# RMSNorm with swish: units of 8 rows in place of 4, one unit per loop round

## The chip, the cores and the metric

The kernel runs on one core of a Trainium2 chip. A core has engines that run side by side, each with its own stream of instructions: TensorE (PE), VectorE (DVE), ScalarE (ACT), GpSimd (POOL) and SyncE (SP). They meet through semaphores. 16 DMA engines move data between the device memory (HBM) and the on-chip memory (SBUF, 128 partitions). The metric is device time in microseconds (us). Lower is better.

## The reference

```python
def reference(x, gamma, eps):            # x: 16 x 1024 x 512 float32, gamma: 512
    rms = np.sqrt(np.mean(x ** 2, axis=-1, keepdims=True) + eps)
    x_norm = x / rms * gamma
    return x_norm * (1.0 / (1.0 + np.exp(-x_norm)))
```

Each of the 16,384 rows of 512 numbers is divided by its own root mean square, multiplied by gamma, and sent through swish (x times its sigmoid). Input and output are 33.55 MB each.

## The kernel before

**Tiling.** Each of the 128 partitions holds 128 rows, so "row r" below means row r of every partition: 128 × 2 KB. SBUF has room for 96 rows in a ring buffer `xb`, and the work is done in place there: a row is loaded, normed, swished and stored from the same spot. Rows 96 to 127 take the place of rows 0 to 31. A *unit* is `cn` = 4 rows, and there are K = 32 of them.

**The five streams.**

- *SyncE* issues all DMAs from one queue, in an order written out by hand (`order`). First the loads of rows 0 to 79 (ten pieces, named by their first row), gamma among them. Then it waits until the load of row 64 has landed ("landed", L167) and issues the store of rows 0 to 31 (L122), then the load of rows 80 to 95 (L116). It waits until that store has finished ("stored") and issues the loads of rows 96 to 127. It waits for the landing of row 112, and issues the other five stores: 32 to 63, 64 to 79, 80 to 95, 96 to 119, 120 to 127. Each store also waits until enough units are finished: `s_swish` must have reached ceil(last row / cn). SyncE takes its instructions in order, so a store that waits holds those behind it.
- *TensorE* multiplies nothing. It carries signals (L177): for unit k it waits for the loads that begin in the unit, and for a sign that the small buffers of unit k - 2 are free, and then counts up `s_land`.
- *ScalarE*, per unit: it waits for `s_land`, squares and sums three of the four rows (one ACTIVATE and one accumulator read each, L219), and then swishes a whole *earlier* unit in one instruction (L227), once VectorE has normed it. It squares two units ahead of the unit that it swishes. The last two units are swished in a single instruction after the loop, which adds 2 to `s_swish` at once.
- *VectorE*, per unit: it sums the squares of the fourth row (L245), and then norms the four rows of the unit before: row × rstd × gamma, one instruction per row (L253).
- *GpSimd*, per unit: it adds eps to the four means (L185), and raises them to the power -1/2 (L190): `rstd`.

So the chain of a unit is: load, squares on ScalarE, the last sum on VectorE, rstd on GpSimd, norms on VectorE, swish on ScalarE, store.

**Loops.** ScalarE and VectorE each run a hardware loop with two units per round (15 rounds); row addresses come from registers, which each round computes anew (fused register operations, L215). GpSimd runs a loop with two units per round as well. Waits inside loops count their semaphore down again (`take`: wait for n, subtract n), so that the waited value stays constant.

Of the kernel before, what the change touches and what calls it, by code (L numbers as in the profile page):

```python
# [9 lines left out]
def kernel(  # L10
# [7 lines left out]
    nc = tc.nc  # L18
    P = nc.NUM_PARTITIONS
    AF = mybir.ActivationFunctionType  # L20
    ALU = mybir.AluOpType
    fp32 = mybir.dt.float32
# [3 lines left out]
    R, D = xf.shape  # L26

    groups = [32, 48, 16, 32]
    ring = 96
# [6 lines left out]
    order += [("stored", 0), ("load", 96), ("load", 112), ("load", 122)]  # L36
    order += [("landed", 112)] + [("store", a) for a in (32, 64, 80, 96, 120)]
    early = 2
    cn = 4

    first = [sum(groups[:g]) for g in range(len(groups))]
    rows_each = sum(groups)
# [6 lines left out]
        assert sum(n for _, n in pieces) == rows_each  # L49

    K = rows_each // cn
    U = 2
    rounds = (K - 2) // U
    assert U * rounds == K - 2
    load_at = {a: t for t, (a, _) in enumerate(loads)}
    store_at = {a: t for t, (a, _) in enumerate(stores)}
    ends = [-(-(a + n) // cn) for a, n in stores]
# [1 line left out]
    inv_d = 1.0 / float(D)  # L59
    eps_f = float(eps)  # L60
# [4 lines left out]
    def sbuf(name, shape, dt=fp32):  # L65
        return nc.alloc_sbuf_tensor(name, shape, dt).ap()

    xb = sbuf("xb", [P, ring, D])
    gamma4 = sbuf("gamma4", [P, D])
    gamma_sb = sbuf("gamma_sb", [P, D])  # L70
    neg_half = sbuf("neg_half", [P, cn])
    ms = [sbuf(f"ms{u}", [P, cn]) for u in range(U)]
    aeps = [sbuf(f"aeps{u}", [P, cn]) for u in range(U)]
    rstd = [sbuf(f"rstd{u}", [P, cn]) for u in range(U)]
    junk = [
        nc.alloc_psum_tensor(f"junk{i}", [P, D], fp32).ap() for i in range(U * (cn - 1))
    ]
    junk_v = [sbuf(f"junk_v{u}", [P, D]) for u in range(U)]

    ld = [nc.alloc_semaphore(f"ld{t}") for t in range(len(loads))]  # L80
    st = [nc.alloc_semaphore(f"st{t}") for t in range(2)]
# [4 lines left out]
    s_land = nc.alloc_semaphore("s_land")  # L86
    s_acc = nc.alloc_semaphore("s_acc")
    s_sum = nc.alloc_semaphore("s_sum")
    s_free = nc.alloc_semaphore("s_free")
    s_eps = nc.alloc_semaphore("s_eps")  # L90
    s_rstd = nc.alloc_semaphore("s_rstd")
    s_norm = nc.alloc_semaphore("s_norm")
# [2 lines left out]
    def need(ins, sem, value):  # L95
        return ins.wait_op(sem, value, "sem-ge")

    def take(queue, sem, n=1):
        queue.wait_ge(sem, n).then_inc(sem, -n)  # L99
# [9 lines left out]
    def buf(piece):  # L109
        a, n = piece  # L110
        at = a % ring
        assert at + n <= ring, piece
        return xb[:, at : at + n, :]

    def load(t):
        return nc.sync.dma_start(  # L116
            out=buf(loads[t]), in_=dram(xf, loads[t])
        ).then_inc(ld[t], 16)
# [25 lines left out]
    for t in range(early):  # L144
        ins = load(t).ins
        assert here[-1] is ins or here[-1].name == ins.name
        here.pop()
        at = next(
            i for i, other in enumerate(entry)
            if other.engine == mybir.EngineType.SP  # L150
            and isinstance(other, mybir.InstDrain)
        )
        entry.insert(at, ins)
    for what, a in order[early:]:
# [4 lines left out]
        elif what == "gamma":  # L159
            need(  # L160
                nc.sync.dma_start(
                    out=gamma4[0:P:32, :], in_=gamma.partition_broadcast(4)
# [10 lines left out]
    for k in range(K):  # L173
        for t, (a, n) in enumerate(loads):
            if k * cn <= a < (k + 1) * cn:
                nc.tensor.wait_ge(ld[t], 16)
        nc.tensor.wait_ge(s_free, max(0, k - U + 1)).then_inc(s_land, 1)  # L177

    nc.gpsimd.memset(gamma4, 0.0).then_inc(s_zero, 1)  # L179
    nc.gpsimd.memset(neg_half, -0.5).then_inc(s_half, 1)  # L180
    nc.gpsimd.wait_ge(s_half, 1)

    def rsqrt(u):
        take(nc.gpsimd, s_sum)
        nc.gpsimd.tensor_scalar(  # L185
            out=aeps[u], in0=ms[u], scalar1=eps_f, scalar2=None, op0=ALU.add,
        ).then_inc(s_eps, 1)
        take(nc.gpsimd, s_eps)
        nc.gpsimd.sem_inc(s_free, 1)
        nc.gpsimd.tensor_tensor(  # L190
            out=rstd[u], in0=aeps[u], in1=neg_half, op=ALU.pow
        ).then_inc(s_rstd, 1)

    rsqrt(0)
    rsqrt(1)
    with nc.gpsimd.Fori(0, rounds, 1):
        for j in range(U):
            rsqrt((2 + j) % U)

    flat = xb.rearrange("p n d -> p (n d)")  # L200
    size = cn * D

    def unit_of(i):
        at = nc.s_assert_within(
            i % (ring * D), 0, ring * D - size,
            skip_runtime_bounds_check_because="whole units, and the ring is whole units",
        )
        return flat[:, bass.ds(at, size)]

    def row_of(unit, r):  # L210
        return unit[:, r * D : (r + 1) * D]

    def addresses(queue, aps):
        for ap in aps:
            queue.lower_ap(ap)  # L215

    def square(u, rows):
        for j in range(cn - 1):
            acc = nc.scalar.activation(  # L219
                out=junk[u * (cn - 1) + j], in_=rows[j], func=AF.Square,  # L220
                scale=inv_d**0.5, accum_out=ms[u][:, j : j + 1],
            )
        acc.then_inc(s_acc, 1)

    def swish(rows, n=1):
        take(nc.scalar, s_norm, n)
        nc.scalar.activation(out=rows, in_=rows, func=AF.Silu).then_inc(s_swish, n)  # L227

    nc.scalar.preload_act_table_set("silu_and_others")  # L229
    take(nc.scalar, s_land, 2)  # L230
    for k in range(2):
        square(k, [xb[:, k * cn + j, :] for j in range(cn)])
    with nc.scalar.Fori(0, rounds * U * size, U * size) as i:
        new = [unit_of(i + (j + 2) * size) for j in range(U)]
        old = [unit_of(i), unit_of(i + size)]
        sq_rows = [[row_of(unit, r) for r in range(cn - 1)] for unit in new]
        addresses(nc.scalar, old + sum(sq_rows, []))
        for j in range(U):
            take(nc.scalar, s_land)
            square((2 + j) % U, sq_rows[j])  # L240
            swish(old[j])
    swish(buf(((K - 2) * cn, 2 * cn)), 2)

    def sums(u, row):
        nc.vector.scalar_tensor_tensor(  # L245
            out=junk_v[u], in0=row, scalar=inv_d, in1=row,
            op0=ALU.mult, op1=ALU.mult, accum_out=ms[u][:, cn - 1 : cn],
        ).then_inc(s_sum, 1)

    def norm(u, rows):  # L250
        take(nc.vector, s_rstd)
        for j in range(cn):
            ins = nc.vector.scalar_tensor_tensor(  # L253
                out=rows[j], in0=rows[j], scalar=rstd[u][:, j : j + 1],
                in1=gamma_sb, op0=ALU.mult, op1=ALU.mult,
            )
        ins.then_inc(s_norm, 1)

    take(nc.vector, s_acc, 2)
    for k in range(2):  # L260
        sums(k, xb[:, k * cn + cn - 1, :])
    need(nc.vector.stream_shuffle(gamma_sb, gamma4, [0] * 32), s_gld, 16).then_inc(  # L262
        s_gamma, 1
    )
    nc.vector.wait_ge(s_gamma, 1)
    norm(0, [xb[:, j, :] for j in range(cn)])
    with nc.vector.Fori(0, rounds * U * size, U * size) as i:
        of_unit = [unit_of(i + (j + 1) * size) for j in range(U + 1)]
        rows = [[row_of(unit, r) for r in range(cn)] for unit in of_unit]
        addresses(nc.vector, sum(rows[:U], []) + rows[U][cn - 1 :])  # L270
        for j in range(U):
            take(nc.vector, s_acc)
            sums((2 + j) % U, rows[j + 1][cn - 1])
            norm((1 + j) % U, rows[j])
    norm((K - 1) % U, [buf(((K - 1) * cn + j, 1))[:, 0, :] for j in range(cn)])


# [33 lines left out]
```

## Time and profile before

| | us |
|---|---|
| median of three runs | 160.26 (159.98 to 161.02) |
| the profiled execution | 160.24 |
| its span, first to last instruction | 158.9 |
| VectorE busy | 107.8 (68%), 194 instructions |
| ScalarE busy | 119.5 (75%), 224 instructions |
| GpSimd busy | 56.7 (36%), 70 instructions |

The largest groups, by line, engine and operation; `out<-in` names the tiles, then come the count, the busy us and the mean ns of one, and the idle time ahead of them with what ended it:

```profile
L253 DVE SCALAR_TENSOR_TENSOR xb<-xb,rstd,gamma_sb 128x512 f32 (+1 forms) x128 | 87.4, 746 | 0.9 <-DVEq L99 0.9
L227 ACT ACTIVATE xb<-xb (+1 forms) x31 | 60.7, 1959 | 6.5 <-ACTq L99 6.5
L219 ACT ACTIVATE junk<-xb 128x512 f32 (+1 forms) x96 | 55.7, 580 | 6.0 <-ACTq L99 6.0
L190 POOL TENSOR_TENSOR rstd<-aeps,neg_half 128x4 f32<-128x4 f32 x32 | 38.7, 1208 | 8.4 <-POOLq L99 8.4
```

DVEq, ACTq, POOLq and SPq are the engines' sequencers, which take the waits; L99 is `take`. The busy tenths divide the span into 40 slices of 4 us; each digit is the busy share of a slice, 9 for 90% or more. Times within the span are counted from its first instruction.

### The profile page before, as it was taken

How to read it: one execution, taken by the hardware profiler on the slowest of the kernel's cores; microseconds unless marked ns; L12 is line 12 of the kernel's file. 1: busy time of each engine (PE TensorE's matmuls, PEld its weight loads, DVE VectorE, ACT ScalarE, POOL GpSimd, SP SyncE). 2: the span in 40 equal slices, each digit the busy share in tenths (PEclk: the TensorE clock that was granted, in tenths of full speed). 3: DMA queues.
4: the chain of work that ended last, by engine and by line, in shares of the span. 5: the costliest groups of instructions: out<-in, count | busy, mean ns of one | idle time of the engine just before them, and what ended most of it. 6: DMA issues, size and time to landing. Idle time of an engine off the chain costs nothing. (4 is left out here: it accounts for less than half of the span.)

```text
span 158.9 us, 1059 instructions
## 1 busy us (share of the span) xinstructions
DVE 107.8 (68%) x194; ACT 119.5 (75%) x224; POOL 56.7 (36%) x70
## 2 busy tenths in 40 slices
DVE  0017989889999999999988999999999970000000
ACT  3174799999999999999999999999999617000000
POOL 1007444444445545555444444554555500000000
DMA  7999999999899969979999899798989999999975
GB/s 258 452 415 450 412 507 412 396 437 487 363 415 542 528 264 528 478 297 412 396 487 429 383 424 601 317 528 379 412 388 404 503 404 404 470 396 520 445 338 214
DMA packets 2744, 67.12 MB, mean 422 GB/s; under 512 B 308, under 2 KB 308, under 8 KB 312
## 3 DMA queue, kind: packets, MB, share of 16 engines
q1 hardware_dynamic: 2744, 67.12, 98.6%
HBM read 33.56 MB, written 33.55 MB: 422 GB/s over the span
## 5 line engine op out<-in xcount | busy, mean ns | idle before, releaser
L253 DVE SCALAR_TENSOR_TENSOR xb<-xb,rstd,gamma_sb 128x512 f32 (+1 forms) x128 | 87.4, 746 | 0.9 <-DVEq L99 0.9
L227 ACT ACTIVATE xb<-xb (+1 forms) x31 | 60.7, 1959 | 6.5 <-ACTq L99 6.5
L219 ACT ACTIVATE junk<-xb 128x512 f32 (+1 forms) x96 | 55.7, 580 | 6.0 <-ACTq L99 6.0
L190 POOL TENSOR_TENSOR rstd<-aeps,neg_half 128x4 f32<-128x4 f32 x32 | 38.7, 1208 | 8.4 <-POOLq L99 8.4
L185 POOL TENSOR_SCALAR aeps<-ms 128x4 f32<-128x4 f32 x32 | 17.3, 541 | 60.4 <-POOLq L99 60.4
L245 DVE SCALAR_TENSOR_TENSOR junk_v<-xb 128x512 f32 (+1 forms) x32 | 22.1, 692 | 21.5 <-DVEq L99 21.5
L219 ACT ACTIVATION_READ_ACCUMULATOR junk<-xb 128x1 f32 x96 | 17.9, 186 | 0.0
L229 ACT ACT_TABLE_LOAD x1 | 1.3, 1283 | 1.9 <-PEq L63 1.9
L245 DVE DVE_READ_ACCUMULATOR junk_v<-xb 128x1 f32 x32 | 2.6, 82 | 0.0
L179 POOL MEMSET gamma<- 128x512 f32 x1 | 0.5, 524 | 1.5 <-POOLq L63 1.5
L262 DVE STREAM_SHUFFLE gamma_sb<-gamma 128x512 f32<-128x512 f32 x1 | 0.7, 715 | 0.0
L292 POOL MEMSET const-float32-0.0<- 128x1 f32 x1 | 0.1, 98 | 0.2 <-issue 0.2
L292 POOL MEMSET const-bfloat16-1.0<- 128x1 bf16 x1 | 0.1, 101 | 0.0
L292 POOL MEMSET const-uint8-127<- 128x1 uint8 x1 | 0.1, 101 | 0.0
L180 POOL MEMSET neg_half<- 128x4 f32 x1 | 0.1, 101 | 0.0
L292 POOL MEMSET const-float32-1.0<- 128x1 f32 x1 | 0.1, 98 | 0.0
L262 DVE LOAD_MASK_SELECT gamma_sb<-gamma x1 | 0.0, 11 | 0.0
## 6 DMA issues: line engine op xcount, KB each, us to landing
xb<-in_x_dram SPq DMA_DIRECT2D x4, 4096.0 KB, 29.8
out_dram<-xb SPq DMA_DIRECT2D x2, 4096.0 KB, 34.3
xb<-in_x_dram SPq DMA_DIRECT2D x3, 2048.0 KB, 13.9
out_dram<-xb SPq DMA_DIRECT2D x1, 6144.0 KB, 28.1
xb<-in_x_dram SPq DMA_DIRECT2D x1, 2816.0 KB, 43.0
xb<-in_x_dram SPq DMA_DIRECT2D x1, 2560.0 KB, 25.1
xb<-in_x_dram SPq DMA_DIRECT2D x2, 1024.0 KB, 5.7
out_dram<-xb SPq DMA_DIRECT2D x1, 2048.0 KB, 24.9
```

The source lines that it names most:

```text
L179: nc.gpsimd.memset(gamma4, 0.0).then_inc(s_zero, 1)
L180: nc.gpsimd.memset(neg_half, -0.5).then_inc(s_half, 1)
L185: nc.gpsimd.tensor_scalar(out=aeps[u], in0=ms[u], scalar1=eps_f, scalar2=None, op0=ALU.add,).then_inc(s_eps, 1)
L190: nc.gpsimd.tensor_tensor(out=rstd[u], in0=aeps[u], in1=neg_half, op=ALU.pow).then_inc(s_rstd, 1)
L219: acc = nc.scalar.activation(out=junk[u * (cn - 1) + j], in_=rows[j], func=AF.Square, scale=inv_d**0.5, accum_out=ms[u][:, j : j + 1],)
L227: nc.scalar.activation(out=rows, in_=rows, func=AF.Silu).then_inc(s_swish, n)
L229: nc.scalar.preload_act_table_set("silu_and_others")
L245: nc.vector.scalar_tensor_tensor(out=junk_v[u], in0=row, scalar=inv_d, in1=row, op0=ALU.mult, op1=ALU.mult, accum_out=ms[u][:, cn - 1 : cn ...
L253: ins = nc.vector.scalar_tensor_tensor(out=rows[j], in0=rows[j], scalar=rstd[u][:, j : j + 1], in1=gamma_sb, op0=ALU.mult, op1=ALU.mult,)
L262: need(nc.vector.stream_shuffle(gamma_sb, gamma4, [0] * 32), s_gld, 16).then_inc(s_gamma, 1)
L292: nc = _bacc.Bacc("TRN2", target_bir_lowering=False, num_devices=1)
```

## The change

A unit becomes 8 rows (`cn` = 8, K = 16), and a loop round of ScalarE and VectorE handles one unit instead of two. Of the 8 rows, ScalarE squares six and VectorE two (`own` = 2); of the first unit, four each (`own_first` = 4). A swish covers 8 rows, 128x4096; the one after the loop still covers the last two units, now 16 rows, 128x8192. The hand-written order and the pieces of the loads and stores stay as they are, and so does the rule ceil(last row / cn) for a store's wait.

GpSimd's loop is written out: 16 pairs of instructions, each waiting on a constant. `rstd` becomes one tile for all rows, which VectorE reads at an address from a register. The sums of unit 0 go to one small tile, `ms[0]`, and those of all later units to the other, `ms[1]`. The sign that a unit's small buffers are free is now GpSimd's `s_eps`, which TensorE reads without counting it down. VectorE's loop starts one unit earlier, with the first unit's norms inside it; per round it computes addresses with nine fused register operations instead of five, ScalarE with three instead of four. One new wait is on ScalarE's own second square, ahead of the second unit.

```diff
-    cn = 4
+    cn = 8
+    own = 2
+    own_first = 4
...
-    rstd = [sbuf(f"rstd{u}", [P, cn]) for u in range(U)]
+    rstd = sbuf("rstd", [P, rows_each])
...
-        nc.tensor.wait_ge(s_free, max(0, k - U + 1)).then_inc(s_land, 1)
+        nc.tensor.wait_ge(s_eps, 0 if k < 2 else k).then_inc(s_land, 1)
...
-    rsqrt(0)
-    rsqrt(1)
-    with nc.gpsimd.Fori(0, rounds, 1):
-        for j in range(U):
-            rsqrt((2 + j) % U)
+    for k in range(K):
+        need(
+            nc.gpsimd.tensor_scalar(
+                out=aeps[k % 2], in0=ms[min(k, 1)], scalar1=eps_f, scalar2=None, op0=ALU.add,
+            ),
+            s_sum, k + 1,
+        ).then_inc(s_eps, 1)
+        need(
+            nc.gpsimd.tensor_tensor(
+                out=rstd[:, k * cn : (k + 1) * cn], in0=aeps[k % 2], in1=neg_half, op=ALU.pow
+            ),
+            s_eps, k + 1,
+        ).then_inc(s_rstd, 1)
...
-    take(nc.scalar, s_land, 2)
-    for k in range(2):
-        square(k, [xb[:, k * cn + j, :] for j in range(cn)])
-    with nc.scalar.Fori(0, rounds * U * size, U * size) as i:
-        new = [unit_of(i + (j + 2) * size) for j in range(U)]
-        old = [unit_of(i), unit_of(i + size)]
-        sq_rows = [[row_of(unit, r) for r in range(cn - 1)] for unit in new]
-        addresses(nc.scalar, old + sum(sq_rows, []))
-        for j in range(U):
-            take(nc.scalar, s_land)
-            square((2 + j) % U, sq_rows[j])
-            swish(old[j])
+    take(nc.scalar, s_land)
+    square(ms[0], junk[cn - own_first :], [xb[:, j, :] for j in range(cn - own_first)])[1].then_inc(s_two, 1)
+    nc.scalar.wait_ge(s_two, 1)
+    take(nc.scalar, s_land)
+    square(ms[1], junk, [xb[:, cn + j, :] for j in range(cn - own)])
+    with nc.scalar.Fori(0, (K - 2) * size, size) as i:
+        new, old = unit_of(i + 2 * size), unit_of(i)
+        sq_rows = [row_of(new, r) for r in range(cn - own)]
+        old_rows = row_of(old, 0, cn)
+        addresses(nc.scalar, [old_rows] + sq_rows)
+        take(nc.scalar, s_land)
+        square(ms[1], junk, sq_rows)
+        swish(old_rows)
     swish(buf(((K - 2) * cn, 2 * cn)), 2)
...
-    take(nc.vector, s_acc, 2)
-    for k in range(2):
-        sums(k, xb[:, k * cn + cn - 1, :])
+    take(nc.vector, s_acc)
+    sums(ms[0], [xb[:, j, :] for j in range(cn - own_first, cn)])
...
-    norm(0, [xb[:, j, :] for j in range(cn)])
-    with nc.vector.Fori(0, rounds * U * size, U * size) as i:
...
-        for j in range(U):
-            take(nc.vector, s_acc)
-            sums((2 + j) % U, rows[j + 1][cn - 1])
-            norm((1 + j) % U, rows[j])
+    with nc.vector.Fori(0, (K - 1) * size, size) as i:
+        new, old = unit_of(i + size), unit_of(i)
+        rows = [row_of(old, r) for r in range(cn)]
+        sum_rows = [row_of(new, r) for r in range(cn - own, cn)]
...
+        factors = [rstd[:, j : rows_each - cn + j + 1][:, bass.ds(at, 1)] for j in range(cn)]
+        addresses(nc.vector, rows + sum_rows + factors)
+        take(nc.vector, s_acc)
+        sums(ms[1], sum_rows)
+        norm(rows, factors)
```

More of the change, by code (lines that the diff above doesn't have):

```diff
@@ L51 @@
     K = rows_each // cn
-    U = 2
-    rounds = (K - 2) // U
-    assert U * rounds == K - 2
     load_at = {a: t for t, (a, _) in enumerate(loads)}
@@ L71 @@
     neg_half = sbuf("neg_half", [P, cn])
-    ms = [sbuf(f"ms{u}", [P, cn]) for u in range(U)]
-    aeps = [sbuf(f"aeps{u}", [P, cn]) for u in range(U)]
-    rstd = [sbuf(f"rstd{u}", [P, cn]) for u in range(U)]
+    ms = [sbuf(f"ms{u}", [P, cn]) for u in range(2)]
+    aeps = [sbuf(f"aeps{u}", [P, cn]) for u in range(2)]
+    rstd = sbuf("rstd", [P, rows_each])
     junk = [
-        nc.alloc_psum_tensor(f"junk{i}", [P, D], fp32).ap() for i in range(U * (cn - 1))
+        nc.alloc_psum_tensor(f"junk{i}", [P, D], fp32).ap() for i in range(cn)
     ]
-    junk_v = [sbuf(f"junk_v{u}", [P, D]) for u in range(U)]
+    junk_v = [sbuf(f"junk_v{j}", [P, D]) for j in range(own_first)]
     ld = [nc.alloc_semaphore(f"ld{t}") for t in range(len(loads))]
@@ L88 @@
     s_sum = nc.alloc_semaphore("s_sum")
-    s_free = nc.alloc_semaphore("s_free")
+    s_two = nc.alloc_semaphore("s_two")
     s_eps = nc.alloc_semaphore("s_eps")
@@ L181 @@
     nc.gpsimd.wait_ge(s_half, 1)
[L183 to L186, printed above, removed]
-        ).then_inc(s_eps, 1)
[L188 to L191, printed above, removed]
-        ).then_inc(s_rstd, 1)
-    rsqrt(0)
-    rsqrt(1)
-    with nc.gpsimd.Fori(0, rounds, 1):
-        for j in range(U):
-            rsqrt((2 + j) % U)
+    for k in range(K):
[4 more added lines that the diff above has]
+            s_sum, k + 1,
+        ).then_inc(s_eps, 1)
+        need(
[3 more added lines that the diff above has]
+            s_eps, k + 1,
+        ).then_inc(s_rstd, 1)
     flat = xb.rearrange("p n d -> p (n d)")
@@ L203, in unit_of @@
     def unit_of(i):
-        at = nc.s_assert_within(
+        return nc.s_assert_within(
             i % (ring * D), 0, ring * D - size,
@@ L207, in unit_of, with row_of @@
         )
-        return flat[:, bass.ds(at, size)]
-    def row_of(unit, r):
-        return unit[:, r * D : (r + 1) * D]
+    def row_of(unit, r, n=1):
+        return flat[:, r * D : ring * D - size + (r + n) * D][:, bass.ds(unit, n * D)]
     def addresses(queue, aps):
@@ L215, in addresses, with square @@
             queue.lower_ap(ap)
[L217 to L221, printed above, removed]
-            )
-        acc.then_inc(s_acc, 1)
+    def square(sums, dummies, rows):
+        done = []
+        for j in range(len(rows)):
+            done.append(
+                nc.scalar.activation(
+                    out=dummies[j], in_=rows[j], func=AF.Square,
+                    scale=inv_d**0.5, accum_out=sums[:, j : j + 1],
+                )
+            )
+        done[-1].then_inc(s_acc, 1)
+        return done
     def swish(rows, n=1):
@@ L229, with sums, norm @@
     nc.scalar.preload_act_table_set("silu_and_others")
-    take(nc.scalar, s_land, 2)
-    for k in range(2):
-        square(k, [xb[:, k * cn + j, :] for j in range(cn)])
-    with nc.scalar.Fori(0, rounds * U * size, U * size) as i:
-        new = [unit_of(i + (j + 2) * size) for j in range(U)]
-        old = [unit_of(i), unit_of(i + size)]
-        sq_rows = [[row_of(unit, r) for r in range(cn - 1)] for unit in new]
-        addresses(nc.scalar, old + sum(sq_rows, []))
-        for j in range(U):
-            take(nc.scalar, s_land)
-            square((2 + j) % U, sq_rows[j])
-            swish(old[j])
-    swish(buf(((K - 2) * cn, 2 * cn)), 2)
[L244 to L250, printed above, removed]
+    take(nc.scalar, s_land)
[11 more added lines that the diff above has]
+        swish(old_rows)
+    swish(buf(((K - 2) * cn, 2 * cn)), 2)
+    def sums(to, rows):
+        n = len(rows)
+        for j in range(n):
+            ins = nc.vector.scalar_tensor_tensor(
+                out=junk_v[j], in0=rows[j], scalar=inv_d, in1=rows[j],
+                op0=ALU.mult, op1=ALU.mult, accum_out=to[:, cn - n + j : cn - n + j + 1],
+            )
+        ins.then_inc(s_sum, 1)
+    def norm(rows, factors):
         take(nc.vector, s_rstd)
@@ L253, in norm @@
             ins = nc.vector.scalar_tensor_tensor(
-                out=rows[j], in0=rows[j], scalar=rstd[u][:, j : j + 1],
+                out=rows[j], in0=rows[j], scalar=factors[j],
                 in1=gamma_sb, op0=ALU.mult, op1=ALU.mult,
@@ L265 @@
     nc.vector.wait_ge(s_gamma, 1)
-    norm(0, [xb[:, j, :] for j in range(cn)])
-    with nc.vector.Fori(0, rounds * U * size, U * size) as i:
-        of_unit = [unit_of(i + (j + 1) * size) for j in range(U + 1)]
-        rows = [[row_of(unit, r) for r in range(cn)] for unit in of_unit]
-        addresses(nc.vector, sum(rows[:U], []) + rows[U][cn - 1 :])
-        for j in range(U):
-            take(nc.vector, s_acc)
-            sums((2 + j) % U, rows[j + 1][cn - 1])
-            norm((1 + j) % U, rows[j])
-    norm((K - 1) % U, [buf(((K - 1) * cn + j, 1))[:, 0, :] for j in range(cn)])
+    with nc.vector.Fori(0, (K - 1) * size, size) as i:
+        new, old = unit_of(i + size), unit_of(i)
+        rows = [row_of(old, r) for r in range(cn)]
+        sum_rows = [row_of(new, r) for r in range(cn - own, cn)]
+        at = nc.s_assert_within(
+            i // D, 0, rows_each - cn,
+            skip_runtime_bounds_check_because="whole units",
+        )
+        factors = [rstd[:, j : rows_each - cn + j + 1][:, bass.ds(at, 1)] for j in range(cn)]
[3 more added lines that the diff above has]
+        norm(rows, factors)
+    k = K - 1
+    norm(
+        [buf((k * cn + j, 1))[:, 0, :] for j in range(cn)],
+        [rstd[:, k * cn + j : k * cn + j + 1] for j in range(cn)],
+    )
 _INS = ['x', 'gamma', 'eps']
```

## The prediction

> **What bounds the kernel now.** I read the page's busy tenths first, then the DMA queue, then SyncE's waits.
>
> ```profile
> DVE  0017989889999999999988999999999970000000
> ACT  3174799999999999999999999999999617000000
> ...
> DMA  7999999999899969979999899798989999999975
> ...
> DMA packets 2744, 67.12 MB, mean 422 GB/s; under 512 B 308, under 2 KB 308, under 8 KB 312
> ...
> q1 hardware_dynamic: 2744, 67.12, 98.6%
> ```
>
> The DMA engines are full from the first slice to the last but one (98.6% of 16 engines), while VectorE and ScalarE stop at 134 us of 158.9. So the span is 67.12 MB through a queue that never runs empty, and compute can only matter where it lets the queue run empty. That happens where SyncE holds a store back:
>
> ```profile
> SPq L167 <- DMA xb<-in_x_dram: 66.3, 2, 42.1
> SPq L122 <- ACT xb L227: 36.2, 4, 21.8
> SPq L171 <- DMA out_dram<-xb: 24.5, 1, 24.5
> ```
>
> The second line is stores waiting for swishes. Whether such a wait hurts is told by the backlog behind it. SyncE's timeline and the DMA view of single windows (issue, then us to landing) give it: the store of rows 80 to 95 is issued at 103.76 and lands 35.8 us later, at 139.5. The next store (rows 96 to 119) is issued at 125.90, 11.8 us before its first packet can move: the packet records show the first engine taking it up at 137.65. The last (rows 120 to 127) is issued at 133.99 and lands at 158.9.
>
> ```profile
> 48.20 0.35 SPq L122 DMA_DIRECT2D out_dram<-xb  x1
> 48.59 23.65 SPq L116 DMA_DIRECT2D xb<-in_x_dram  x4
> 96.51 37.81 SPq L122 DMA_DIRECT2D out_dram<-xb  x5
> ```
>
> ```profile
> 124.84 5.38 DVE L253 SCALAR_TENSOR_TENSOR xb<-xb,rstd,gamma_sb 128x512 f32 x8
> ...
> 125.90 8.42 SPq L122 DMA_DIRECT2D out_dram<-xb  x2
> ...
> 130.35 3.62 ACT L227 ACTIVATE xb<-xb 128x4096 f32<-128x4096 f32 x1 [4.47 <-ACTq L99]
> ```
>
> One more resource is tight. The load of rows 80 to 95 is issued at 48.59 behind the first store and lands 32.0 us later, at 80.6. TensorE, which hands landed rows to ScalarE (L177), waited on it: its longest wait, 2,832 ns, is that one; it starts at 77.8.
>
> ```profile
> xb<-in_x_dram SPq DMA_DIRECT2D x1, 4096.0 KB, 32.0
> ```
>
> ```profile
> L177 PEldq EVENT_SEMAPHORE  x32: 51/51/2832, 2.0 to 118.5; - x32
> ```
>
> ScalarE wanted those rows at about 81.5 (its rounds are 3.69 us apart, from 44.60 on), so it lost nothing.
>
> **The change, part by part.**
>
> *Round of 8 rows.* ScalarE before, per 8 rows: 44.60 to 51.98, 7.38 us. After: six squares at 0.612 (45.21 to 45.83) and one swish of 4,096 elements, 3.62 us as in the last swish above, less the 0.11 by which the next instruction starts before a swish ends: 3.67 + 3.51 = 7.18. VectorE: two sums at 0.61 and eight norms at 0.66 (5.38 for eight, above) are 6.5; its loop with ScalarE, over two rounds, is swish 3.51, squares 3.58 to the last accumulator read, 0.34 to VectorE, 1.23, 5.39, and 0.13 back to ScalarE: 14.2, or 7.1 a round. So ScalarE sets the round: 7.18, a gain of 0.2 us per 8 rows. GpSimd does half as many pairs. Power over 8 elements instead of 4 lies between 1.21 us (the row at 4) and 2.4 (double); beside a norm of 5.4 us either is free. The removed semaphore steps stood in front of nothing that waits. The register work per VectorE round (in the trace 1.06 us for five fused operations, add and branch; now nine, about 1.75 us) runs while norms already handed over are executing, so I cost it at nothing; the price without that cover is in the rivals.
>
> *Start.* Unit 1 needs the load of rows 8 to 15, which lands at 12.2 (issued 1.91, 10.3 to landing). Six squares from 12.37 end at 16.15, the two sums end at 17.5, norm 0 (rstd is there by 15.9 even with the doubled power) at 22.9, swish 0 begins at 23.05. It did 17.01 for half a unit before. Three rounds of 7.18 later swish 3 begins at 44.6 and ends at 48.2: rows 0 to 31 were ready at 44.7 before. The first store goes at 48.2 in the old trace, held by the landing of rows 64 to 74 (L167). So 3.4 us of cover are used up, just. Load packets keep the engines busy to 50.24, so with 1.0 to 1.5 us from issue to packet (below) an issue up to about 49 costs nothing. I take nothing, and keep 1.0 us as the other end: a round's 1.75 us of register work exposed once, less 0.8 of cover.
>
> *Look-ahead.* ScalarE squares two units ahead, now 16 rows instead of 8. Unit 10 (row 80) is wanted after swish 7, at 44.6 + 4 × 7.18 + 3.5 = 76.8, but its load lands at 80.6 as before. ScalarE idles 4.0 us, and all that the shorter rounds gave is waited away there. It restarts at 80.8.
>
> *The end of compute.* From 80.8 five rounds lead to the squares of unit 15: 80.8 + 5 × 7.18 = 116.7. Squares and accumulator 3.77, to VectorE 0.15, two sums 1.23: 121.85. Then norms 14 and 15 back to back, 15 × 0.66 + 0.75 = 10.7: 132.5. Then 0.13 and the last swish, now two units of 8 rows, 8,192 elements: 1.90 for 2,048 and 3.62 for 4,096 are 1.71 per 2,048 more, so 7.04. Compute ends at **139.7** (before: 134.0).
>
> *What waits for it.* The code lets the store of rows 96 to 119 go at ceil(120/8) = 15 finished units. The loop finishes 14, the last swish adds two at once. So this store, 24 rows, goes with the last one at 139.7, not at 125.9; behind it in SyncE's queue stands only the last store. The store of rows 80 to 95 goes at 109.6 instead of 103.8, under the two stores that keep the engines busy until 129.8; free. So the queue runs empty from 137.65 on (the first engine; the last is done at 139.0) until the first packets of the held store.
>
> *From issue to first packet* no row shows this place. The nearest is the first load, the only issue into idle engines: issued at 0.00, first packets between 1.01 and 1.54 on the 16 engines. The upper end is the first store, issued at 48.20 with first packet at 50.24, behind other packets: 2.04. I take 1.5, the last engine of the nearest row, because the last engine ends the kernel. [...]
>
> *Sum.* The 32 rows left took 14.5 us (24 rows, landing 139.5 to 154.0) and 4.9 us (154.0 to 158.9): 19.4. From the last packet to the end of the span 0.5. So 139.7 + 1.5 + 19.4 + 0.5 = 161.1 against 158.9: +2.2 us. The profiled execution took 160.24 with a span of 158.9, 1.34 outside it, and the median of the three runs is 160.26, the same. Predicted: 161.1 + 1.34 = **162.5**. With 1.0 or 2.04 for the issue: 161.9 and 163.0. About 1% (1.6 us) is what a measurement of this kernel can tell from no change, so the forecast lies just beyond it.
>
> **Rivals.**
>
> *The queue covers the late store (not slower).* Time 160.2. It decides at one point: compute must end by 137.65 - 1.3 = 136.3. It would if unit 10 did not wait: 139.7 - 4.0 = 135.7. For it: only 3.4 us separate the cases. Against: the load of row 80 moves in the same full queue behind the same store, and lands at 80.6 unless that changes. 0.12.
>
> *The held store starts quickly.* The first load is also the first DMA of the program; a later one may reach idle engines sooner. [...] Against: the row shows 1.01 to 1.54. 0.07.
>
> *VectorE becomes the bound.* If its queue takes few instructions ahead, part of the 1.75 us of register work per round is exposed. All of it: (14.2 + 1.75) / 2 = 8.0 a round, 0.8 more, five times: 166.4; half: 164.4. Against: before, the register work began 0.2 us after the four norms were handed over, all four still ahead of the engine; three norms cover 1.75 us. 0.10.
>
> *The first store is late.* If swish 3 ends after 49, each us is lost at once and moves every later transfer, the load of row 80 too: up to 1.0, 163.0 to 163.5. For it: the start is a chain of five estimates with 0.8 us of cover. 0.06.
>
> *Faster.* The engines carry the same bytes and were already full; under 158.7 needs a higher rate. 0.02.
>
> **How the numbers follow.** Forecast 0.63 (161.9 to 163.2), covered 0.12, quick start 0.07, VectorE 0.10, late first store 0.06, faster 0.02.
>
> The range 161.2 to 164.6 leaves out the covered case, the faster one, and the upper half of the VectorE case: about 0.19. Faster by over 1%: 0.02. Within 1% (up to 161.86): the covered case and the quick start, 0.19. Slower: 0.79.
>
> **What would show it.** In the profile after: TensorE's longest wait grows to some 5 us and still ends at 80.6; ScalarE idle some 4.0 us there; rounds 7.2 us apart; last swish of 7.0 us ending near 139.7; the last two stores issued within 0.5 us of each other; DMA tenths with a hole near 138 to 141, full on both sides; ScalarE's busy time down by about 4 us, to no use. I am wrong if there is no hole, if the load of row 80 lands at another time, or if the rounds are longer than 7.4.

## The result, and the profile after

| us | before | after |
|---|---|---|
| median (6 runs each) | 160.18 (159.95 to 161.02) | 161.74 (161.64 to 162.38) |
| profiled execution, and its span | 160.24, 158.9 | 161.80, 160.5 |
| instructions in the span | 1059 | 847 |

The ratio is 1.0097, with a 95% interval of 1.0070 to 1.0125: slower by 1.56 us, between 1.1 and 2.0. A fifth fewer instructions run, ScalarE works 4.0 us less, and the kernel takes longer.

From the page of the changed kernel, the busy tenths of ScalarE and of the DMA engines, and the DMA queue:

```profile
ACT  3159389999999999999189999999998009700000
...
DMA  7999999999999997969999999969979999299997
...
q1 hardware_dynamic: 2744, 67.12, 97.7%
```

The digit 2 near the end of the DMA row, 136.4 to 140.4 us, is new; digits of 6 and 7 stood in the row of before as well. The digit 1 in the middle of ScalarE's row is its wait for row 80. SyncE's waits and timeline:

```profile
SPq L166 <- DMA xb<-in_x_dram: 66.1, 2, 42.0
SPq L121 <- ACT xb L225: 42.0, 2, 29.7
...
SPq L170 <- DMA out_dram<-xb: 20.0, 1, 20.0
```

```profile
48.15 0.35 SPq L121 DMA_DIRECT2D out_dram<-xb  x1
48.53 23.66 SPq L115 DMA_DIRECT2D xb<-in_x_dram  x4
96.39 44.03 SPq L121 DMA_DIRECT2D out_dram<-xb  x5
```

The waits of stores for swishes were 36.2 us in four pieces and are 42.0 in two; the longest, 29.7 us, is the store of rows 96 to 119, which now stands until the last swish ends. The five last stores were issued over 37.8 us and are issued over 44.0. The end of compute, in order of time (16 norms, the last swish, the last two stores):

```profile
121.75 10.69 DVE L255 SCALAR_TENSOR_TENSOR xb<-xb,rstd,gamma_sb 128x512 f32 x16
...
132.56 7.03 ACT L225 ACTIVATE xb<-xb 128x8192 f32<-128x8192 f32 x1 [8.69 <-ACTq L98]
139.62 0.81 SPq L121 DMA_DIRECT2D out_dram<-xb  x2
```

And the wait in the middle, on ScalarE (the squares of unit 10 after swish 7) and on TensorE, whose longest wait is 4,920 ns:

```profile
73.25 3.60 ACT L225 ACTIVATE xb<-xb  x1
80.66 0.60 ACT L215 ACTIVATE junk<-xb 128x512 f32 x1 [3.81 <-ACTq L98]
```

```profile
L176 PEldq EVENT_SEMAPHORE  x16: 51/51/4920, 7.3 to 115.4; - x16
```

By the packet records the 16 engines finished the store of rows 80 to 95 between 137.6 and 138.5, and took up the held store between 140.45 and 140.60. Before, they went from the one to the other without a pause, between 137.65 and 139.03.

### The profile page after: what moved, and what is told of

It is laid out like the page before. It is cut to its first block, busy times and chain, and to the rows that moved or that the text cites. A ratio compares the mean times of both kernels' runs of the same rounds, so it can differ in the third digit from the quotient of the medians.

```text
span 160.5 us, 847 instructions
## 1 busy us (share of the span) xinstructions
DVE 107.6 (67%) x198; ACT 115.5 (72%) x204; POOL 42.9 (27%) x38
## 5 line engine op out<-in xcount | busy, mean ns | idle before, releaser
L255 DVE SCALAR_TENSOR_TENSOR xb<-xb,rstd,gamma_sb 128x512 f32 (+1 forms) x128 | 86.1, 746 | 0.0
L225 ACT ACTIVATE xb<-xb (+1 forms) x15 | 57.5, 3834 | 9.4 <-ACTq L98 9.4
L215 ACT ACTIVATE junk<-xb 128x512 f32 (+1 forms) x94 | 54.7, 582 | 12.8 <-ACTq L98 12.8
L189 POOL TENSOR_TENSOR rstd<-aeps,neg_half 128x8 f32<-128x8 f32 x16 | 31.8, 1985 | 1.3
L183 POOL TENSOR_SCALAR aeps<-ms 128x8 f32<-128x8 f32 x16 | 10.3, 647 | 78.8 <-DVE junk_v L246 78.8
## 6 DMA issues: line engine op xcount, KB each, us to landing
xb<-in_x_dram SPq DMA_DIRECT2D x4, 4096.0 KB, 29.7
```

What stands on the lines that cost most here:

```text
L183: nc.gpsimd.tensor_scalar(out=aeps[k % 2], in0=ms[min(k, 1)], scalar1=eps_f, scalar2=None, op0=ALU.add,),
L189: nc.gpsimd.tensor_tensor(out=rstd[:, k * cn : (k + 1) * cn], in0=aeps[k % 2], in1=neg_half, op=ALU.pow),
L215: nc.scalar.activation(out=dummies[j], in_=rows[j], func=AF.Square, scale=inv_d**0.5, accum_out=sums[:, j : j + 1],)
L255: ins = nc.vector.scalar_tensor_tensor(out=rows[j], in0=rows[j], scalar=factors[j], in1=gamma_sb, op0=ALU.mult, op1=ALU.mult,)
```

## The experiments

All changes are against the changed kernel, but for the third. "Before" in each is the kernel before, on the same chip.

**Cut the last swish in two.** Does the release of the held store carry the loss?

```diff
-    swish(buf(((K - 2) * cn, 2 * cn)), 2)
+    for k in (K - 2, K - 1):
+        swish(buf((k * cn, cn)))
```

> The changed kernel with the last swish cut in two, one for each of the last two units. Theory (the held store of rows 96 to 119 is the whole loss): unit 14 is normed at 127.1 in the trace of the changed kernel, so its swish ends at 130.9 and the store goes there, 6.5 us before the first DMA engine is free (137.4). No hole; the time is that of before, 160.2. Rival (the loss lies in the loading or in the rate of the transfers, or in the rounds of 8): it stays at 161.7.

Measured 160.23, ratio to before 1.0002 (0.9980 to 1.0023): the whole loss is gone.

```profile
127.19 3.62 ACT L225 ACTIVATE xb<-xb 128x4096 f32<-128x4096 f32 x1 [3.39 <-ACTq L98]
130.84 5.63 SPq L121 DMA_DIRECT2D out_dram<-xb  x2
132.49 3.62 ACT L225 ACTIVATE xb<-xb 128x4096 f32<-128x4096 f32 x1 [1.68 <-ACTq L98]
```

The held store goes at 130.84, as worked out, and the page has 98.8% for the DMA queue. Everything else of the change is still in: the rounds of 8, the written-out GpSimd loop, the wait for row 80. Together these cost and gain nothing that can be measured.

**Cut the load of rows 80 to 95 in two.** Would the coarse release hurt if compute ended earlier?

```diff
-    loads += [(80, 16), (96, 16), (112, 10), (122, 6)]
+    loads += [(80, 8), (88, 8), (96, 16), (112, 10), (122, 6)]
...
-    order += [("landed", 64), ("store", 0), ("load", 80)]
+    order += [("landed", 64), ("store", 0), ("load", 80), ("load", 88)]
```

> The changed kernel with the load of rows 80 to 95 cut into two loads of 8 rows, next to each other in the same place of the queue. Theory: rows 80 to 87 then land at 70.9 + 4.8 = 75.7, before ScalarE wants them at 76.8, so its wait of 4.0 us goes, compute ends at 135.6 instead of 139.6, the held store's first packet could come at 136.5, 0.9 us before the first engine is free: 160.2. Rival (the release at the last swish costs by itself, whatever ScalarE waited for before): 161.7.

Measured 159.81, ratio 0.9983 (0.9966 to 1.0000). ScalarE's swishes 7 and 8 are now one round apart, where they were 11.1 us apart in the changed kernel:

```profile
73.25 3.61 ACT L225 ACTIVATE xb<-xb  x1
80.43 3.61 ACT L225 ACTIVATE xb<-xb  x1
```

The held store still goes with the last swish, at 135.70, 3.9 us earlier. The engines were busy until 137.6 at least, and the loss is gone again. So the loss needs both: the release of 24 rows with the last swish, and the wait for row 80 that makes the last swish late. Either mend is enough.

**The coarse release alone**, in the kernel before:

```diff
     ends = [-(-(a + n) // cn) for a, n in stores]
+    ends[store_at[96]] = K
```

> The kernel before, with nothing changed but that the store of rows 96 to 119 waits for all 32 units, as it in effect does in the changed kernel. Theory: it goes at 134.0 instead of 125.9, its first packet could come at 134.9, the engines are busy until 137.6: 160.2, no change. The coarse release alone costs nothing; it needs the late end of compute. Rival (a release with the last store costs by itself): 161 or more.

Measured 160.08, ratio 1.0004 (0.9980 to 1.0029). The store is issued at 134.0 instead of 125.9, 8 us later, and this costs nothing that can be measured.

**A later end of compute.** How much is a microsecond worth beyond that point?

```diff
-    swish(buf(((K - 2) * cn, 2 * cn)), 2)
+    take(nc.scalar, s_norm, 2)
+    for j in range(4):
+        nc.scalar.activation(out=junk[j], in_=xb[:, 40 + j, :], func=AF.Silu)
+    tail = buf(((K - 2) * cn, 2 * cn))
+    nc.scalar.activation(out=tail, in_=tail, func=AF.Silu).then_inc(s_swish, 2)
```

> The changed kernel with four idle swishes of 128x512 (results thrown away) between the norms of the last two units and their swish. By the rows of the changed kernel (0.58 each, the next beginning 0.09 before the end) they put the end of compute off by about 2.0 us. Theory: past the point where the queue runs empty each us of compute is a us of time: 163.7, with a hole of about 4.6 us in the DMA, and 0.8 us from the issue of the held store to its first packet again. Rival (the end is set elsewhere): 161.7.

Measured 163.86, ratio 1.0222 (1.0194 to 1.0250). The end of compute, and the end of its DMA row, where the hole is now a whole slice:

```profile
132.59 2.15 ACT L243 ACTIVATE junk<-xb 128x512 f32<-128x512 f32 x4 [8.69 <-ACTq L98]
134.69 7.01 ACT L245 ACTIVATE xb<-xb 128x8192 f32<-128x8192 f32 x1
141.72 0.81 SPq L121 DMA_DIRECT2D out_dram<-xb  x2
```

```profile
DMA  7999999989999999999999999999799898099897
```

The stores go 2.11 us later than in the changed kernel (141.72 against 139.62), and the median is 2.12 us higher. One for one. First packets again come 0.83 to 0.98 us after the issue, and from issue to the last landing it is 20.8 us in both.

**The load ahead of the first store.** The other way to end the wait for row 80, and a second look at an issue into idle engines:

```diff
-    order += [("landed", 64), ("store", 0), ("load", 80)]
+    order += [("load", 80), ("landed", 64), ("store", 0)]
```

> The changed kernel with the load of rows 80 to 95 issued ahead of the first store instead of behind it. Theory: it lands near 61, ScalarE never waits for it, compute ends near 136, and the hole before the held store goes. But the first store then finishes near 80.5 with nothing queued behind it, and SyncE issues the load of row 96 only then: a new hole, from the last packet of the store, near 80.0, to the first packet of that load. It also measures the time from issue to first packet for a load into idle engines in mid-run: 0.83 as for the held store of the changed kernel, or 1.01 as for the first load of the program. Time 160.1 + 1.2 = 161.3. Rival (the wait for row 80 was the only loss, the order is free): 160.1.

Measured 163.36, ratio 1.0226 (1.0194 to 1.0259): 3.4 us above before, where 1.2 was expected. The hole at the end is gone, as expected: the held store goes at 137.83, while the engines are busy until 141.5. Compute ends there and not at 136, because TensorE now waits 3.3 us for row 96, until 93.1. The hole in the middle is there, but dearer than worked out:

```profile
48.17 0.35 SPq L121 DMA_DIRECT2D out_dram<-xb  x1
81.13 1.28 SPq L115 DMA_DIRECT2D xb<-in_x_dram  x3
99.33 39.90 SPq L121 DMA_DIRECT2D out_dram<-xb  x5
```

The last packets of the first store end between 80.2 and 80.8. The load goes when the store's landing has been reported, at 81.13. Its first packets start between 82.08 and 82.96, so an engine idles about 2 us, and they take 1.2 to 2.1 us where such a packet takes 1.21 in a full queue. That is some 2.5 us, where the span is 3.0 us longer than before (161.9 against 158.9). The packet records show that the rest is a balance. In this run packets are also slow shortly before the queue passes from one kind of transfer to the other: the last ones of rows 80 to 95, from 57.4 on, take up to 2.1 us, and those of rows 122 to 127, near 100, up to 1.06 where 0.46 is usual. That is 1.0 and 0.7 us more on the mean of the engines; before loses 0.2 in this way, at 67. Against it the engines idle 0.8 us less at the end and lose 0.2 less at the start. So the order costs more than its hole; why those packets are slow stays open.

**A late start.** What cover had the first store?

```diff
+    nc.scalar.activation(out=xb[:, 88:92, :], in_=xb[:, 0:4, :], func=AF.Silu)
     square(ms[1], junk, [xb[:, cn + j, :] for j in range(cn - own)])
```

> The changed kernel with one idle swish of 128x2048 (1.8 us, its result thrown away) on ScalarE between the squares of unit 0 and of unit 1. It puts off swish 3, and with it the first store, from 48.1 to 49.9. Theory: with 0.83 us from issue to first packet the store was free until 49.3 (the first engine runs out of loads at 50.1), so 0.3 to 0.7 us are lost there and handed on to everything later: the load of row 80 lands near 81.0, ScalarE waits 2.6 us for it instead of 4.0, compute ends near 140.1: 162.2. Rival (no cover at the first store): 161.7 + 1.8 = 163.5. Rival (the wait at row 80 swallows all of it): 161.7.

Measured 162.71, ratio 1.0172 (1.0159 to 1.0186): 1.0 us over the changed kernel by the medians and 1.2 by the ratios, where 0.5 was expected; the rivals had 0 and 1.8. This one alone does not choose well between them; the trace does.

```profile
49.77 0.35 SPq L121 DMA_DIRECT2D out_dram<-xb  x1
50.16 22.64 SPq L115 DMA_DIRECT2D xb<-in_x_dram  x4
97.17 44.03 SPq L121 DMA_DIRECT2D out_dram<-xb  x5
```

The store goes 1.62 us later than in the changed kernel. Its packets start from 50.61 on, and the engines ran out of loads between 50.19 and 50.67: 0.3 us idle on the mean. Row 80 lands at 81.3, 0.8 later, the last stores go 0.8 later, and the end is 0.8 later in the profile. So half of the delay was covered, and what was lost there was handed on in full to the end, unswallowed by the wait at row 80. The 0.8 is more than the 0.3 of idling because the store itself ran longer: on the mean of the engines it begins 0.25 us later than in the changed kernel and ends 0.88 later. Its last packet on each engine, from 67.6 on, took 2.9 to 3.5 us where such a packet usually takes 2.42; in the changed kernel five of these 16 took over 2.6, at most 2.9. Why they are slow, no run here shows.

**Both mends together** (the last swish and the load each cut in two):

> The changed kernel with both mends: the last swish cut in two and the load of rows 80 to 95 cut in two. Theory: compute ends near 132, the held store goes near 127, but the DMA engines are full either way: 160.0, not faster than either mend alone. Rival (there is still something to win from shorter rounds): 159 or less.

Measured 160.09, ratio 1.0011 (0.9989 to 1.0034). Compute ends at 132.1, 1.8 us earlier than in the kernel before:

```profile
126.86 5.63 SPq L121 DMA_DIRECT2D out_dram<-xb  x2
128.52 3.62 ACT L225 ACTIVATE xb<-xb 128x4096 f32<-128x4096 f32 x1 [1.68 <-ACTq L98]
```

Nothing comes of it. Its DMA queue is at 99.0% (98.6% before). No version here beats the kernel before beyond its interval.

## Why the prediction was nearly right

The direction, the mechanism and the place were right; the size was 2.2 us where 1.56 came. (The terms of the sum add to 162.44, which the forecast gives as 162.5.) I called that slower by more than 1%; it is 0.97%, with an interval on both sides of 1%, so it belongs to the "within 1%" that I gave less.

| step | predicted | measured |
|---|---|---|
| swish 0 begins; swish 3 ends | 23.05; 48.2 | 22.95; 48.11 |
| first store issued | 48.2 | 48.15 |
| round of 8 rows on ScalarE | 7.18 | 7.18 |
| row 80 lands; ScalarE's wait for it | 80.6; 4.0 | 80.5; 3.8 |
| squares of unit 15 begin | 116.7 | 116.59 |
| last swish, 8,192 elements | 7.04 | 7.03 |
| compute ends | 139.7 | 139.59 |
| issue of the held store to the last engine's first packet | 1.5 | 0.98 |
| from there to the end of the span | 19.9 | 19.9 |

*The step that failed* is the one from issue to first packet. I took 1.5 us, the last engine of the first load of the program, because it was the only issue into idle engines. The held store's first packets came after 0.83 to 0.98 us. That is sooner than the 1.01 of the first load and comes near the rival of the quick start, to which I had given 0.07. By my sum 0.9 gives 161.8, within 1%, and 0.98 gives 161.9; compute also ended 0.1 us earlier, the profiled execution took 161.80, and the median lies 0.06 under it. The later readings suggest why the row that I leaned on did not carry over: it was a load. The loads into idle engines started over a wide spread, 1.01 to 1.54 us after the issue at the program's start (in the trace of before) and 0.95 to 1.83 in mid-run (in the fifth experiment); the held stores of two traces started within 0.15 us of each other, both from 0.83 to 0.98. Sizes and places differ too, and only one load was caught in mid-run, so that the direction makes the difference is not shown. The runs have 0.83 at the earliest into idle engines; with 1.5 I predicted 162.5, and 161.74 was measured.

*The queue covers the late store* did not happen, and the second experiment shows that its condition was the right one: with row 80 in time it does happen.

*VectorE becomes the bound* did not happen. In a round near 74 us the register work begins at 74.04, while the first sum is still in work and a second sum and all eight norms have been handed over, and it ends at 75.6; the norms run to 80.1. So VectorE had ten instructions in hand at that point, the accumulator reads of the sums not counted; the trace shows one of them executing and does not tell where the other nine stood.

*The first store is late* did not happen either. The store now goes with swish 3 (48.11), 0.1 us after the landing of row 64 (48.03), and is issued when it was before (48.15 against 48.20); the sixth experiment shows that some 0.8 us of cover remained (1.62 us later there, 0.8 at the end), and that what is lost beyond it is handed on.

*What the removed work was worth.* ScalarE was ready for row 80 at 76.9 and waited 3.8 us for it, so what the shorter rounds had saved up to there was waited away. The last experiment shows the gain at its best: compute 1.8 us shorter, time the same. The power over 8 elements took 1.99 us (1.21 over 4), between the bounds, beside the norms.

## What to carry to other kernels

Where the DMA queue is full from end to end, as here (98.6% before the change), read compute only for the moments at which it releases transfers, and set each issue against the time at which the queue would run dry. A larger unit of work rounds these releases up and asks for its input earlier; here neither cost anything alone, and the two together opened a hole. Part of it was slack of the engines; once it was open, 2.11 us more of compute cost 2.12 us. It can be mended where the release is, by a finer last step, with the large unit kept everywhere else.

## What the hardware showed that was not expected

After the hole the 16 engines ran in step. Before, they took up the last big store over 1.4 us (137.65 to 139.03) and ended over 1.3 (157.1 to 158.4); after the hole they started within 0.15 us and ended within 0.16. The fourth experiment shows the same (0.15 and 0.15). The kernel ends with its slowest engine, so part of an engine's idle time was slack already: a typical engine stood idle 2.7 us (137.8 to 140.5), and the span grew by 1.6.

In these traces a load into idle engines cost more than a store. The first packets of the load of row 96 in the fifth experiment took up to 2.07 us instead of 1.21 and started over 0.9 us; those of the held store took 1.87 instead of 1.82 and started over 0.15.
